# Three small edits around the first expert round: a sort product moved, slots handed on in another order, one slot more

## The chip, the core and the metric

One core of a Trainium2 chip runs the whole program. TensorE (PE) multiplies matrices and writes to PSUM banks; VectorE (DVE) and ScalarE (ACT) empty the banks; GpSimd (POOL) does some elementwise work; SyncE (SP) issues the weight transfers, and 16 DMA engines carry them. The metric is the device time of one execution in microseconds (us). The time before is the median of 3 runs.

## The reference

Two layers over 512 tokens of width 1024. Each layer mixes tokens (dilated attention, a spatial gating unit, a short convolution), then runs a mixture of 32 experts of which each token uses two of one group:

```python
def hierarchical_moe(x, wg, bg, we, be, w_gate, w_up, w_down):
    ...
    _, g_idx = lax.top_k(g_logit, 1)
    ...
    top_logit, top_local = lax.top_k(e_logit, TOP_K_INNER)
    gate = g_p * jax.nn.softmax(top_logit, -1)
    expert = g_idx * EXPERTS_PER_GROUP + top_local
    ...
    def run_block(args):
        rows, e = args
        xb = x_pad[rows]
        hdn = jax.nn.silu(xb @ w_gate[e]) * (xb @ w_up[e])
        return hdn @ w_down[e]
```

All weights are float32. An expert has three matrices of 2 MB, so the 32 experts of a layer are some 200 MB, and every one of them is read.

## The kernel before, in words

Each layer has a dense stage (`dense`, `output`) and an expert stage (`moe`). In the expert stage the experts are worked off in 13 rounds. Rounds 0 and 1 are fixed: each serves two experts that are known beforehand, 64 columns of tokens for each. Rounds 2 to 12 take the other 28 experts, in an order that the kernel finds by sorting the experts by their token counts. The sort is `keys`, `sort_a`, `sort_b`, `sort_c`: `sort_a` ranks the experts with two small products on TensorE; `sort_b` makes a table `found` on VectorE and ends with a product (L1226) that spreads it over all partitions; `sort_c` copies the result into `ids`, `base` and `cap`. `ids` tells SyncE which experts to load from round 2 on.

These steps are woven into `gather`, which collects the tokens of rounds 0 and 1 on TensorE in four quarters (L1334), each into one of two `t` banks, emptied half by ScalarE (L1345) and half by VectorE (L1343).

The weights live in slots of 1 MB. `self.free` is a list of the names of the free slots, first in, first out. `feed` takes the next entries of a fixed loading order while slots are free and issues their transfers on SyncE's queue (L362 for the experts); an issued transfer waits on the queue until the former content of its slot has been read, and all behind it wait too. `drop` and `release` give a weight's slots back to the list:

```python
    def drop(self, *keys):
        ws = [self.loaded.pop(key) for key in keys]
        for tags in zip(*(w.tags for w in ws)):
            self.give(tags)
```

Each weight has two slots, its first and its second half. The loading order of a fixed round is: first halves of gate of both experts, first halves of up, second halves of gate, second halves of up. `first(r)` is a round's product with gate and up (through `hidden`, L1374); for a fixed round `hidden` is called with `parts` ((0, 4), (4, 8)), so it reads in that same order. `second(r)` is the product with down (L1405). The program order is: gathers and sort, `first(0)`, `first(1)`, `second(0)`, the gathers of round 2 and 3, `second(1)`, and then round by round. Two further slots, named Y and Z, hold dense tiles and serve once per layer for a weight.

In the expert stage the order of all engines is as the code is written (`self.manual`); in most of the dense stage a planner of the framework orders the instructions. At the end of the dense stage `output` gives back the last dense slots and feeds.

Of the kernel before, what the change touches and what calls it, by code (L numbers as in the profile page):

```python
# [28 lines left out]
NE = 32  # L29
# [46 lines left out]
def columns(members):  # L76

    w = 64 if all((b - a) % 64 == 0 for _, a, b in members) else 32
    return [(e, c, c + w) for e, (_, a, b) in enumerate(members) for c in range(a, b, w)]
# [86 lines left out]
class Trunk:  # L166
# [4 lines left out]
    def setup(self, ctx):  # L171
        tc, nc = self.tc, self.nc
        con = ctx.enter_context(tc.tile_pool(name="con", bufs=1))
        self.slots = ctx.enter_context(tc.tile_pool(name="slots", bufs=1))
        self.ps = ctx.enter_context(tc.tile_pool(name="ps", bufs=1, space=PSUM))
        self.sm = ctx.enter_context(tc.tile_pool(name="sm", bufs=2))

        self.X = con.tile([128, NT, D], F32, name="X")
        self.fa = con.tile([128, 4, 512], FR, name="fa")
        self.f = con.tile([128, 8, 512], F32, name="f")  # L180
        self.tab = con.tile([128, NTAB - 512], F32, name="tab")
        self.ident = con.tile([128, 128], F32, name="ident")
        self.tri = con.tile([128, 128], BF, name="tri")
        self.onesb = con.tile([128, 128], BF, name="onesb")
        self.ones = con.tile([128, 128], F32, name="ones")
        self.eps = con.tile([128, 1], F32, name="eps")
        self.pp = con.tile([128, NPP], F32, name="pp")
        self.wr = con.tile([128, KT + 1, 64], F32, name="wr")
        self.rk = con.tile([128, NT, NE], F32, name="rk")
        self.G = con.tile([128, NT, NE], F32, name="G")  # L190


        self.u = con.tile([128, R0, NT], F32, name="u")
        self.Gp = con.tile([128, R0, NT], F32, name="Gp")
        self.ur = con.tile([128, 2, NT, NS], F32, name="ur")
        self.base = con.tile([128, NE], F32, name="base")
        self.ids = con.tile([128, NE], I32, name="ids")
        self.gt = con.tile([128, 2, 512], F32, name="gt")
        self.cap = con.tile([128, NE], F32, name="cap")
        self.cnt = con.tile([128, 96], I32, name="cnt")  # L200
        self.gv1 = con.tile([128, 1], F32, name="gv1")


        self.fb = self.half("fb", FR, "Y")[0]
        self.f2 = self.half("f2", F32, "Z")[0]
        m = 0
        self.iota = self.tab[:, m : m + 128]
        self.perm = self.tab[:, m + 164 : m + 196]
        self.w4 = self.tab[:, m + 128 : m + 132]
        self.w32 = self.tab[:, m + 132 : m + 164]  # L210
        col = lambda c: self.tab[0:NE, m + c : m + c + 1]
        self.t_at, self.t_base, self.t_cap, self.t_id, self.t_tie = (col(c) for c in range(196, 201))
        self.t_ties = self.tab[:, m + 201 : m + 233]
        self.t_rounds = self.tab[:, m + 233 : m + 233 + NS]

        for t in range(2):
            self.load_x(t)
        make_identity(nc, self.ident)
        nc.gpsimd.memset(self.onesb, 1.0)
        nc.gpsimd.memset(self.ones, 1.0)  # L220
        nc.gpsimd.memset(self.eps, EPS)
        nc.gpsimd.affine_select(
            out=self.tri, in_=self.onesb, pattern=[[1, 128]], compare_op=OP.is_gt,
            fill=0.0, base=0, channel_multiplier=-1,
        )
        self.free = [f"R{k}" for k in range(18)]

    def load_x(self, t):
        self.nc.sync.dma_start(self.X[:, t, :], self.i["x"][t * 128 : (t + 1) * 128, :])
# [986 lines left out]
    def sort_b(self):  # L1216

        v, rt, rp = self.nc.vector, self.rt, self.rp
        self.found = rt[0:NE, 472:568]
        at = rt[0:NE, 470:471]  # L1220
        v.tensor_copy(at, rp[0:NE, 240:241])
        row = rp[0:NE, 200:232]
        v.tensor_scalar(self.found[:, 64:96], self.iota[0:NE, 0:32], at, self.t_id, OP.is_equal, OP.mult)
        v.tensor_scalar(self.found[:, 0:32], row, self.t_at, self.t_base, OP.is_equal, OP.mult)
        v.tensor_scalar(self.found[:, 32:64], row, self.t_at, self.t_cap, OP.is_equal, OP.mult)
        self.nc.tensor.matmul(self.rp[:, 256:352], self.ones[0:NE, :], self.found, start=True, stop=True)  # L1226

    def sort_c(self):

        v, ps = self.nc.vector, self.rp[:, 256:352]  # L1230
        v.tensor_copy(self.ids, ps[:, 64:96])
        v.tensor_copy(self.base, ps[:, 0:32])
        v.tensor_copy(self.cap, ps[:, 32:64])
# [81 lines left out]
    def moe(self, l):  # L1315
        nc, f, fa = self.nc, self.f, self.fa
# [7 lines left out]
        def gather(quarters=range(4), n=2):  # L1324

            w = 128 * n
            for kk in quarters:
                ps = self.t()
                for j in range(2):
                    k = 2 * kk + j  # L1330
                    i = 0
                    for src, one in ((x1h, oh), (x1l, self.oh16)):
                        for t in range(NT):
                            nc.tensor.matmul(  # L1334
                                ps[:, w * j : w * j + w], src[:, k, 128 * t : 128 * t + 128],
                                one[:, 0:n, t, :], start=(i == 0), stop=(i == 2 * NT - 1),
                            )
                            i += 1
                for j in range(2):
                    k = 2 * kk + j  # L1340
                    src = ps[:, w * j : w * j + w]
                    if j:
                        nc.vector.tensor_scalar(xg[:, k, 0:w], src, gain(k), bias(k), OP.mult, OP.add)  # L1343
                    else:
                        nc.scalar.activation(xg[:, k, 0:w], src, AF.Identity, bias=bias(k), scale=gain(k))  # L1345
# [16 lines left out]
        def members(r):  # L1362
            return len(ROUNDS[r - R0] if r >= R0 else FIXED[r])

        def weights(r, *names):
            return [self.loaded[(l, n, r, e)] for n in names for e in range(members(r))]

        def hidden(pss, w, xs, blocks, fill=(), parts=((0, 8),)):

            fill = list(fill)  # L1370
            for m, part in [(m, part) for part in parts for m in range(len(w))]:
                for k in range(*part):
                    for e, a, b in blocks:
                        nc.tensor.matmul(  # L1374
                            pss[m][a:b, :], xs[:, k, a:b], w[m][e][:, k, :],
                            start=(k == 0), stop=(k == 7),
                        )
                    if k % 2 == 1 and fill:
                        fill.pop(0)()
# [166 lines left out]
        def release(r, *names):  # L1546
            for n in names:
                self.drop(*((l, n, r, e) for e in range(members(r))))

        def first(r, fill=(), keep=0):  # L1550

            pss = [self.g(), self.g()]
            xs = xg[:, :, 128 * (r % 2) : 128 * (r % 2) + 128]
            if r >= R0:
                for m, n in enumerate(("gate", "up")):
                    if m:
                        self.feed()
                    hidden(pss[m:], [weights(r, n)], xs, columns(ROUNDS[r - R0]), fill[4 * m : 4 * m + 4])
                    release(r, n)
            else:  # L1560
                w = [weights(r, n) for n in ("gate", "up")]
                hidden(pss, w, xs, halves, fill, ((0, 4), (4, 8)))
                release(r, "gate", "up")
            if keep == 1:
                spare.append(self.free.pop())
            held = [self.free.pop() for _ in range(4 if keep == 4 else 0)]
            self.feed()
            self.free.extend(held)
            return pss
# [23 lines left out]
        with self.manual(ET.PE, ET.SP):  # L1593

            gather((0,))
            self.sort_a()
            gather((1,))
            self.sort_b()
            gather((2,))
            self.sort_c()  # L1600
            self.known = l
            self.feed()
# [9 lines left out]
            slots = []  # L1612
            none = lambda: None
            pss = first(0, [none] * 5 + [lambda: slots.append(by_slot(0)), none, lambda: slots.append(by_slot(1))])
            h = act(pss)
            self.gates(2)
# [16 lines left out]
            for r in range(R0, NR):  # L1633
# [3 lines left out]
                n = min(2, NR - 1 - r)  # L1637
# [48 lines left out]
        n = 4 // members(NR - 1)  # L1686
# [165 lines left out]
```

## Time and profile before

| | |
|---|---|
| time before, median of 3 runs | 1522.19 us (1519.39 to 1522.41) |
| time of the profiled execution | 1520.52 us |
| its span, first to last instruction | 1518.8 us |
| TensorE busy | 1368.6 us (90%) |
| VectorE busy | 683.3 us (45%) |
| DMA, mean over the span | 293 GB/s |

The profile is of one execution. A busy time is the time in which an engine worked on any instruction. SyncE's queue (SPq) isn't counted as busy; its waits are listed apart, counted from the end of its last instruction. A wait names what ended it. PEclk is the granted TensorE clock: 1.00 is 2.4 GHz, 0.50 is 1.2 GHz.

### The profile page before, as it was taken

The numbers are of one execution on the slowest core, as the hardware profiler recorded it, in microseconds if no ns is written. First come the engines' busy times: TensorE is split into PE (matmuls) and PEld (weight loads), VectorE is DVE, ScalarE is ACT, GpSimd is POOL, SyncE is SP. The second block draws the span as 40 slices with busy tenths as digits, with TensorE's granted clock in tenths as the row PEclk, the third lists the DMA queues.
The fourth block names the chain that finished last, engine by engine and source line by source line (L and its number), as shares of the span: only waits on it lengthen the run. The fifth ranks groups of instructions, "written<-read, shape, count | busy, mean of one in ns | idle before, by whom it ended". The sixth has DMA issues, their size and how long they took to land. (4 is left out here: it accounts for less than half of the span.)

```text
span 1518.8 us, 22582 instructions
## 1 busy us (share of the span) xinstructions
PE 1368.6 (90%) x8828; PEld 750.3 (49%) x8829; DVE 683.3 (45%) x1528; ACT 397.2 (26%) x720; POOL 156.0 (10%) x190
## 2 busy tenths in 40 slices
PE   8999997999989898989699998979999898989894
PEld 7776576443434342434377665864434343433341
DVE  4347758534242424232553676585352424241325
ACT  5446544110101010101463555341101010101013
POOL 2112206000000000000141221060000000000001
PEclk9999999899999998999799998999999999999997
DMA  9410354499999999999911025444999999999994
GB/s 346 141 56 1 113 193 166 164 411 408 419 419 419 418 419 410 419 418 410 382 45 59 1 84 192 141 167 184 410 410 419 419 418 419 419 410 419 419 404 151
DMA packets 84551, 445.16 MB, mean 293 GB/s; under 512 B 8080, under 2 KB 14352, under 8 KB 36816
## 3 DMA queue, kind: packets, MB, share of 16 engines
q1 hardware_dynamic: 83184, 440.15, 72.2%
q0 software_dynamic: 960, 2.90, 0.6%
q8 instruction: 74, 1.21, 0.3%
q10 hardware_dynamic: 288, 0.52, 0.1%
q14 instruction: 45, 0.37, 0.1%
HBM read 441.45 MB, written 2.10 MB: 292 GB/s over the span
## 5 line engine op out<-in xcount | busy, mean ns | idle before, releaser
L1374 PE MATMUL g<-w,f 128*32 128x512 f32 (+1 forms) x3072 | 411.8, 602 | 36.3 <-DMA w<-expert_w_up 26.9
L1374 PEld LDWEIGHTS g<-w,f 128*32 128x32 f32 (+1 forms) x3072 | 113.6, 113 | 303.5 <-issue 220.6
L1405 PE MATMUL g<-w,f 128*32 128x512 f32 (+1 forms) x1536 | 215.4, 642 | 31.3 <-DMA w<-expert_w_down 15.6
L1405 PEld LDWEIGHTS g<-w,f 128*32 128x32 f32 (+1 forms) x1536 | 58.8, 118 | 165.0 <-issue 125.3
L1416 DVE SCALAR_TENSOR_TENSOR y<-g,gv,y 128x512 fp32r<-128x512 f32 x52 | 39.1, 751 | 208.8 <-ACT y L1415 206.4
L1428 DVE TENSOR_TENSOR X<-X,s 128x512 f32<-128x512 f32 x88 | 56.4, 683 | 127.1 <-PE s L1423 127.1
L1415 ACT ACTIVATE y<-g,gv 128x512 fp32r<-128x512 f32 x52 | 35.8, 689 | 245.0 <-PE g L1405 245.0
L1334 PE MATMUL t<-fa,mh 128*128 128x256 f32 (+1 forms) x448 | 82.8, 308 | 0.6 <-DVE f L1207 0.6
L1387 DVE TENSOR_TENSOR f<-g,f 128x512 f32<-128x512 f32 x26 | 17.9, 690 | 134.3 <-PE g L1374 130.9
L1345 ACT ACTIVATE f<-t,pp 128x256 f32<-128x256 f32 (+1 forms) x56 | 30.9, 551 | 177.1 <-PE t L1334 177.1
L1343 DVE TENSOR_SCALAR f<-t,pp 128x256 f32<-128x256 f32 (+1 forms) x56 | 29.4, 525 | 90.8 <-ACT f L1345 90.8
L1334 PEld LDWEIGHTS t<-fa,mh 128*128 128x128 f32 x448 | 62.7, 197 | 12.4 <-DVE X L1428 8.4
L1334 PE MATMUL t<-f,x1l 128*128 128x256 f16 (+1 forms) x448 | 67.5, 275 | 0.0
L1428 DVE TENSOR_TENSOR X<-X,t 128x512 f32<-128x512 f32 x88 | 56.3, 682 | 19.9 <-PE t L1423 19.9
L1423 PE MATMUL s<-y,fa 128*128 128x512 f32 x208 | 62.8, 422 | 2.4 <-ACT y L1415 1.8
L1386 ACT ACTIVATE f<-g 128x512 f32<-128x512 f32 x26 | 15.6, 598 | 188.3 <-PE g L1374 188.3
L1534 POOL DMA_DIRECT2D rows<-ln_gain x2 | 1.1, 550 | 586.9 <-PEq L1450 586.9
L1423 PEld LDWEIGHTS s<-y,fa 128*128 128x128 f32 x208 | 35.0, 188 | 51.2 <-issue 40.1
L1423 PE MATMUL t<-y,fa 128*128 128x512 f32 x208 | 59.1, 405 | 0.5 <-DVE xl L462 0.5
L1394 ACT COPY f<-s 128x512 f32<-128x512 f32 x26 | 15.2, 587 | 162.9 <-PE s L1393 135.1
L409 POOL TENSOR_TENSOR X<-X,E 128x512 f32<-128x512 f32 x11 | 16.3, 1486 | 332.5 <-ACT X L1712 168.8
L409 POOL TENSOR_TENSOR X<-X,f 128x512 f32<-128x512 f32 x32 | 40.9, 1309 | 87.8 <-DVE x1l L953 82.3
(343 smaller groups left out, 2273.8 us busy)
## 6 DMA issues: line engine op xcount, KB each, us to landing
w<-expert_w_gate SPq DMA_DIRECT2D x128, 1024.0 KB, 19.8
w<-expert_w_up SPq DMA_DIRECT2D x128, 1024.0 KB, 19.8
w<-expert_w_down SPq DMA_DIRECT2D x116, 1024.0 KB, 19.8
w<-w_in SPq DMA_DIRECT2D x20, 1024.0 KB, 13.9
w<-expert_w_down SPq DMA_DIRECT2D x48, 256.0 KB, 5.4
w<-w_out SPq DMA_DIRECT2D x8, 1024.0 KB, 5.5
X<-x SPq DMA_DIRECT2D x4, 512.0 KB, 5.8
w<-w_in SPq DMA_DIRECT2D x4, 512.0 KB, 8.1
```

Source lines behind the costliest of these rows:

```text
L409: e.tensor_tensor(out=x, in0=x, in1=row[:, 512 * h : 512 * h + 512], op=op)
L1334: nc.tensor.matmul(ps[:, w * j : w * j + w], src[:, k, 128 * t : 128 * t + 128], one[:, 0:n, t, :], start=(i == 0), stop=(i == 2 * NT - 1),)
L1343: nc.vector.tensor_scalar(xg[:, k, 0:w], src, gain(k), bias(k), OP.mult, OP.add)
L1345: nc.scalar.activation(xg[:, k, 0:w], src, AF.Identity, bias=bias(k), scale=gain(k))
L1374: nc.tensor.matmul(pss[m][a:b, :], xs[:, k, a:b], w[m][e][:, k, :], start=(k == 0), stop=(k == 7),)
L1386: nc.scalar.activation(hp, gate, AF.Silu)
L1387: nc.vector.tensor_mul(hp, up, hp)
L1405: nc.tensor.matmul(pss[hf][a:b, :], hT[:, 128 * j + a : 128 * j + b], part(e, hf, j), start=(j == 0), stop=(j == 3),)
L1415: nc.scalar.mul(yh, ps, gv)
L1416: nc.vector.scalar_tensor_tensor(yl, ps, gv, yh.bitcast(F32), OP.mult, OP.subtract)
L1423: nc.tensor.matmul(ps, oT[:, 128 * t : 128 * t + 128], y[q], start=(q == 0), stop=(q == 1))
L1428: nc.vector.tensor_add(x, x, ps)
```

## The change

Three edits. The list of slots has 19 names instead of 18; the 8 KB per partition for it come in part from a smaller scratch for the transfers that GpSimd issues (`dynamic_dma_scratch_size`, 8192 to 2048 bytes). The product of L1226 moves from the end of `sort_b` to the head of `sort_c`, and `sort_b` now stands ahead of the second quarter of the gather: TensorE's order goes from quarter 0, `sort_a`, quarter 1, product, quarter 2, quarter 3 to quarter 0, `sort_a`, quarters 1 and 2, product, quarter 3. And a fixed round gives its gate and up slots back in one `drop`, so that the list gets the first halves of gate and up before the second halves.

```diff
-        self.free = [f"R{k}" for k in range(18)]
+        self.free = [f"R{k}" for k in range(19)]
...
         v.tensor_scalar(self.found[:, 32:64], row, self.t_at, self.t_cap, OP.is_equal, OP.mult)
+
+    def sort_c(self):
+
         self.nc.tensor.matmul(self.rp[:, 256:352], self.ones[0:NE, :], self.found, start=True, stop=True)
-
-    def sort_c(self):
-
         v, ps = self.nc.vector, self.rp[:, 256:352]
...
                 hidden(pss, w, xs, halves, fill, ((0, 4), (4, 8)))
-                release(r, "gate", "up")
+                self.drop(*((l, n, r, e) for n in ("gate", "up") for e in range(members(r))))
...
             gather((0,))
             self.sort_a()
-            gather((1,))
             self.sort_b()
-            gather((2,))
+            gather((1, 2))
             self.sort_c()
...
-    nc = bacc.Bacc("TRN2", target_bir_lowering=False, num_devices=1, dynamic_dma_scratch_size=8192)
+    nc = bacc.Bacc("TRN2", target_bir_lowering=False, num_devices=1, dynamic_dma_scratch_size=2048)
```

## Rows read from the trace of the kernel before

**Rows 1.** The page: the span, and the DMA engines' busy tenths in 40 slices.
```profile
span 1518.8 us, 22582 instructions
...
DMA  9410354499999999999911025444999999999994
```

**Rows 2.** Windows: stretch, busy us (instructions) by engine, PEclk, DMA share, GB/s.
```profile
265.00:285.50 20.50, 17.83 (x103) 13.21 (x104) 8.30 (x39) 3.78 (x8) 1.00 (x2) 0.79 0.01 2
...
302.80:400.00 97.20, 96.97 (x706) 44.30 (x706) 41.17 (x86) 13.93 (x23) 0.00 (x0) 1.00 1.01 412
...
310.00:740.00 430.00, 392.00 (x2871) 163.01 (x2867) 146.33 (x287) 48.52 (x80) 1.06 (x2) 0.96 1.01 414
```

**Rows 3.** TensorE's waits, 400 to 735 us: total us, times, longest.
```profile
PE g L1374 <- DMA w<-expert_w_up: 12.5, 11, 1.5
PE g L1405 <- DMA w<-expert_w_down: 9.1, 6, 2.3
```

**Rows 4.** SyncE's waits: 284:286, 286:293, 320:345; last row 1040:1048, layer 1.
```profile
SPq L362 <- PE g L1374: 37.2, 1, 37.2
...
SPq L362 <- PE g L1374: 6.0, 1, 6.0
...
SPq L362 <- PE g L1405: 17.4, 2, 12.8
...
SPq L362 <- PE g L1374: 35.9, 1, 35.9
```

**Rows 5.** Timeline of SyncE's issues in layer 0: start us, us, count.
```profile
285.54 11.37 SPq L362 DMA_DIRECT2D w<-expert_w_down  x7
...
292.40 4.50 SPq L362 DMA_DIRECT2D w<-expert_w_down  x5
297.71 0.35 SPq L362 DMA_DIRECT2D w<-expert_w_gate  x1
...
338.18 0.90 SPq L362 DMA_DIRECT2D w<-expert_w_down  x2
...
338.74 0.33 SPq L362 DMA_DIRECT2D w<-expert_w_down  x1
```

**Rows 6.** Single issues at 285.54, 292.40, 297.71, 338.74: us to landing at the end.
```profile
w<-expert_w_down SPq DMA_DIRECT2D x1, 1024.0 KB, 5.0
...
w<-expert_w_down SPq DMA_DIRECT2D x1, 1024.0 KB, 4.9
...
w<-expert_w_gate SPq DMA_DIRECT2D x1, 1024.0 KB, 13.2
...
w<-expert_w_down SPq DMA_DIRECT2D x1, 1024.0 KB, 7.9
```

**Rows 7.** Timeline of the gather stage, layer 0: start us, us, idle before, releaser.
```profile
274.58 0.54 DVE L1343 TENSOR_SCALAR f<-t,pp 128x256 f32<-128x256 f32 x1 [2.01 <-ACT f L1345]
...
275.98 0.46 PE L1226 MATMUL g<-f,ones 32*128 32x96 f32 x2 [2.39 <-DVE f L1225]
...
281.86 4.51 PE L1374 MATMUL g<-w,f 128*64 128x512 f32 x20
```

**Rows 8.** Windows of the gather stage; the last is layer 1's.
```profile
273.56:276.97 3.41, 1.02 (x8) 0.85 (x8) 1.31 (x5) 0.57 (x1) 0.00 (x0) 1.00 0.01 2
276.98:280.39 3.41, 3.41 (x19) 2.85 (x17) 0.00 (x0) 0.57 (x1) 0.00 (x0) 0.50 0.00 0
...
1034.74:1038.15 3.41, 3.41 (x19) 2.85 (x17) 0.41 (x1) 0.57 (x1) 0.00 (x0) 0.50 0.00 0
```

**Rows 9.** TensorE's waits in layer 1, 1026 to 1040 us.
```profile
PE g L1226 <- DVE f L1225: 2.1, 1, 2.1
```

**Rows 10.** The view of line 444: who waited for it, and its loads' landings.
```profile
  ACT f L875: 7.4, 2
...
DMA to landing us min/median/max: 4.0/5.9/7.0
```

## The prediction

> **What bounds the kernel now.** I began with the page's row of DMA shares over the span: it is at its top in two long stretches and low between them [rows 1]. These stretches are the expert rounds of the two layers. The windows of layer 0 show the border: from 265 to 285.5 us the DMA engines move 2 GB/s while TensorE works, from 310 to 740 us they are full at 414 GB/s, and TensorE is busy for 392 of those 430 us [rows 2]. So one transfer of 1.0486 MB takes 1.0486/0.414 = 2.53 us there. The table of TensorE's waits from 400 to 735 us says what its idle time waits for: weights that land, 12.5 us for up and 9.1 us for down [rows 3]. Between 302.8 and 400 us TensorE itself never rests, 96.97 of 97.20 us [rows 2]; from 400 us on it runs behind the weights. The end of a layer's rounds is therefore the start of the weight stream, plus the number of transfers still to come times 2.53 us, plus the holes in the stream, plus a tail that the change leaves alone. The stream starts where SyncE's queue gets its first free slot: it sits 37.2 us in layer 0 and 35.9 us in layer 1 until `hidden` (L1374) has read the first quarter of fixed round 0 [rows 4]. All three edits act at this place.
>
> **The change part by part.**
>
> *The sort's last product.* In the gather stage TensorE stands 2.39 us before the product of L1226, because VectorE makes its operand only after the second quarter's evacuation at 274.58 us [rows 7]. In the new order VectorE's four small steps of `sort_b` come ahead of that evacuation; they are ready once the first quarter is evacuated, and the 2.01 us in which VectorE was idle ahead of 274.58 hold their 0.9 us (they ran between that evacuation's end at 275.1 and the product's start at 275.98 [rows 7]). TensorE goes on with the third quarter, then takes the product (0.46 us, as before), then the fourth. The two t banks do not hold it: the third quarter wants the bank of the first, the fourth that of the second, evacuated at 274.58 + 0.54 = 275.1 us [rows 7], earlier than TensorE gets there. The three copies of `sort_c` wait for the third quarter's evacuation on VectorE; behind them are the fourth quarter's evacuation and `gating`, which move up with TensorE all the same. SyncE's `feed` there issues nothing, as no slot is free, and the expert numbers are first needed for the gate load at 297.71 us [rows 5]. So the wait goes: 2.39 us in layer 0, 2.1 us in layer 1 [rows 9].
>
> The rest is the clock. In the stretch with the wait TensorE was busy for 1.02 of 3.41 us, and in the next 3.41 us the granted clock was 0.50, 1.2 instead of 2.4 GHz, although TensorE was busy throughout; layer 1 shows the same stretch at 0.50 [rows 8]. These were gather matmuls, so 3.41 us at half clock is work of 1.7 us. With no rest ahead of it I take the clock to stay up: 1.7 us more. If it falls all the same, the gain of this part is the wait alone. Part one moves the first matmul of the rounds, now at 281.86 us [rows 7], and with it the first released slot, by 2.4 + 1.7 = 4.1 us in layer 0 and 2.1 + 1.7 = 3.8 us in layer 1.
>
> *The nineteenth slot.* Counting through `feed`, `take` and `give`, 17 of a layer's 24 fixed transfers are issued before the stall with 18 slots (the two dense tiles Y and Z serve once as well), and 18 with 19. The extra transfer runs in the stretch where the DMA engines are idle [rows 2], so the stream after it is one transfer shorter: 2.5 us. That holds in both layers; in the dense stages the extra slot waits for an unlimited `feed`, and loads that come earlier there have no one waiting for them.
>
> *Reading order.* `hidden` reads the fixed rounds in quarters: first halves of gate, of up, second halves of gate, of up. Before, the slots go back as gate, gate, gate, gate, up, up, up, up, so the third transfer waits for the third quarter (SyncE stands 6.0 us [rows 4], until 292.40 [rows 5]) while the slots of the second quarter lie free. The cost is read from the landings. The first transfer is issued at 285.54 and lands 5.0 us later, at 290.5; the eighth is the gate load of 297.71, which lands 13.2 us later, at 310.9 [rows 5, 6]. Seven steps of 2.53 us would give 290.5 + 17.7 = 308.2, so the hole costs 2.7 us. With the new order a quarter takes (292.40 - 285.54)/2 = 3.4 us; the second quarter's slots are free at 289.0 and their first load could land at 289.0 + 4.9 = 293.9 [rows 6], before its turn at 295.6. The third quarter's, 292.40 + 4.9 = 297.3, are before theirs at 300.6. The hole closes.
>
> *What is given back.* Slot and order together put the stream 2.5 + 2.7 = 5.2 us ahead of TensorE's own timetable, and there is a later place where slots are released by TensorE: the down matrices of fixed round 1 (L1405), where SyncE already stands up to 12.8 us [rows 4]. As each transfer takes the slot of the one before it in the list, the load issued at 338.74 and landed 7.9 us later, at 346.6, now needs the slot released at 338.18; it cannot land before 338.18 + 4.9 = 343.1 [rows 5, 6]. So 3.5 of the 5.2 us survive. TensorE is full in this stretch [rows 2], so its releases move by part one alone. Past 400 us its 38 us of rest in 430 [rows 2] take the 3.5 us in.
>
> The Trainium skill, page "DMA: Bandwidth & Descriptors", section "Where 436 GB/s comes from", lets the HBM side bind loads at some 358 GB/s per core. The windows show 414 GB/s [rows 2], and the measurement decides. By the page one transfer would take an estimated 2.9 us and the slot would be worth 0.4 us more in each layer.
>
> *The smaller scratch* serves the loads that GpSimd issues. No row shows them at the new size. Those of L444 land 4.0 to 7.0 us after issue [rows 10], and I take no cost, which is what these rows show at the old size: the lower bound is nothing, the upper one is the last rival.
>
> *Sum.* Layer 0: 4.1 + 3.5 = 7.6. Layer 1: 3.8 + 3.5 = 7.3. Together 14.9 us. The profiled execution took 1520.52 us (span 1518.8), 1.7 below the median 1522.19 and inside the runs' 1519.39 to 1522.41. 1520.5 - 14.9 = 1505.6; against the median it would be 1507.3. I say 1505.5.
>
> **The rivals.**
>
> *The clock falls all the same.* TensorE also rests ahead of the gathers, and the wait may not be what costs the clock. Against it: the stretch at 0.50 comes right behind the one with the rest [rows 8]. Then part one is 2.4 and 2.1: 14.9 - 3.4 = 11.5, 1509.
>
> *A new wait for the one removed.* If the third quarter or the moved product waits on an evacuation, part one gives nothing; for it speaks that TensorE has only two t banks and VectorE empties half of each quarter; against it the bank times above. The rest is 2 x 3.5 = 7.0: 1513.5.
>
> *All of the 5.2 us is kept.* If the releases of round 1 come earlier than by part one, 2 x 1.7 = 3.4 more: 18.3, 1502.2. TensorE's full stretch speaks against it.
>
> *Hidden.* If TensorE and not the stream set the end of the rounds, nothing changes, 1520.5. For it: 392 of 430 us busy [rows 2]. Against it: the rest is waits for weights [rows 3].
>
> *Slower: GpSimd's loads in pieces.* ScalarE's scaling at L875 waits 7.4 us in two for the row load of L444 [rows 10], and ScalarE's evacuations for the output stage are queued behind it. If a scratch of a quarter cuts that load into four pieces, each waiting for the last to land, it lands 3 x 7.0 = 21 us later in each layer; TensorE waits for those evacuations, and the time is 1520.5 - 14.9 + 42 = 1548. It decides from 7.5 us of delay per layer on. Against it: at the old size the same loads show no sign of pieces, 4.0 to 7.0 us being about what SyncE's loads take (5.0 and 4.9 us [rows 6]).
>
> The Trainium skill, page "SBUF — State Buffer", section "SBUF size: 192, 224, or 256?", has 16 KiB per partition set aside for these descriptor rings, which speaks against 2 KiB. No run here shows that size; before ran with 8 KiB and the landings above.
>
> **How the numbers follow.** Forecast 0.60; clock falls 0.13; new wait 0.09; all kept 0.06; hidden 0.06; slower 0.06. The range takes in the forecast, the clock, the new wait and the larger gain, with a spread of 1 to 2 us between executions: 1501 to 1514. About 0.2% (3 us) is what a measurement here can tell from no change; faster holds 0.60 + 0.13 + 0.09 + 0.06 = 0.88, same 0.06, slower 0.06.
>
> **What the changed profile would show.** Part one: no wait before L1226, granted clock 1.00 through the fourth quarter, the first L1374 of the rounds 4 us earlier against the gathers' start. Slot: two down loads instead of one before the stall. Order: SyncE's 6.0 us wait after the first release shrinks to about 3, and the loads behind it land every 2.53 us. Given back: a longer wait on L1405 near the release of round 1's down slots. It would be wrong if TensorE waited less for weights past 400 us and the rounds still ended no earlier, if the dense stages, which a planner orders and in which every slot name moves by one, came out longer, or if L875 waited longer.

## The result, and the profile after

The changed kernel took 1511.18 us (median of 4 runs, 1507.70 to 1512.29), the kernel before beside it 1521.45 us (4 runs). The ratio is 0.993, 95% interval [0.991, 0.9951]: 7.5 to 13.7 us faster. The prediction said 1505.5 us in a range of 1501 to 1514. The profiled execution is that of 1512.29 us, the slowest of the four, with a span of 1510.5.

The gather stage first. Windows of layer 0 (columns as in [rows 2]), in the place of [rows 8]:

```profile
271.82:275.23 3.41, 3.41 (x31) 2.88 (x28) 1.31 (x5) 0.56 (x1) 0.00 (x0) 0.99 0.02 5
275.24:278.65 3.41, 3.41 (x29) 2.87 (x27) 1.20 (x5) 1.13 (x2) 0.00 (x0) 1.00 0.01 2
278.65:282.06 3.41, 3.41 (x22) 1.68 (x22) 1.65 (x10) 0.87 (x3) 0.00 (x0) 1.00 0.00 0
```

The timeline of the same stretch, in the place of [rows 7] (the product now stands in L1229), and TensorE's waits from 268 to 284 us, all that there are:

```profile
270.43 1.19 PE L1334 MATMUL t<-fa,mh 128*128 128x256 f32 x4 [0.27 <-DVE f L1207]
...
277.25 0.46 PE L1229 MATMUL g<-f,ones 32*128 32x96 f32 x2
...
279.69 4.51 PE L1374 MATMUL g<-w,f 128*64 128x512 f32 x20
```

```profile
PE t L1334 <- DVE f L1207: 0.3, 1, 0.3
```

From the second to the fourth quarter TensorE is busy without a gap, the product has no wait, and the granted clock stays at 2.4 GHz (the first quarter still begins at the low clock, as the 1.19 us of its first four matmuls show). From the first gather matmul to the first matmul of the rounds it takes 9.26 us where before took 13.47.

Now SyncE, in the place of [rows 4]: the waits from 282 to 284, from 284 to 291 and from 318 to 345 us. In the block below them are the landings of single issues, at 283.37 (the first into a handed-on slot), 330.35, 336.00 and 336.58 us, in the place of [rows 6].

```profile
SPq L362 <- PE g L1374: 32.2, 1, 32.2
...
SPq L362 <- PE g L1374: 4.8, 2, 2.6
...
SPq L362 <- PE g L1405: 17.4, 2, 12.8
```

```profile
w<-expert_w_down SPq DMA_DIRECT2D x1, 1024.0 KB, 5.0
...
w<-expert_w_down SPq DMA_DIRECT2D x1, 1024.0 KB, 4.9
...
w<-expert_w_down SPq DMA_DIRECT2D x1, 1024.0 KB, 5.0
...
w<-expert_w_down SPq DMA_DIRECT2D x1, 1024.0 KB, 8.1
```

The wait of 6.0 us became two of 2.6 and 2.2. The wait of 12.8 us for the down matrices of round 1 is unchanged, and now the two loads issued when it and the next one end (330.35 and 336.00) land 4.9 and 5.0 us later, about the least that an expert load of 1 MB took in any profile here (4.8). Before, the load issued at the end of the wait of 12.8 us took 5.8.

To see what the stream of weights kept of its gains, I count a layer's 210 expert loads in their order and take for each the time from the first issue into a handed-on slot to its landing. The *lead* is how much less that is than for the same load of before. Part one does not enter it; the other two edits do. (Each value is a difference of landing times of the trace; layer 0, layer 1.)

| kernel | 25th load | 36th | 39th | 41st | last |
|---|---|---|---|---|---|
| changed kernel | 4.3, 4.5 | 4.3, 4.3 | 3.4, 1.0 | 2.6, 1.2 | 2.8, 1.0 |
| changed kernel, again | 4.2, 4.3 | 4.2, 4.4 | 3.4, 3.3 | 2.4, 2.4 | 2.3, 2.7 |
| scaling moved | 4.4, 4.2 | 4.4, 4.3 | 3.5, 3.2 | 2.6, 1.9 | 2.6, 1.7 |
| move alone | -0.1, 0.0 | -0.2, -0.1 | -0.1, 0.0 | 0.2, 0.3 | 0.1, 0.4 |
| slot and scratch alone | 2.4, 2.6 | 2.4, 2.1 | 3.2, 2.3 | 2.4, 2.4 | 2.7, 2.8 |
| order alone | 1.7, 1.9 | 0.2, 1.1 | -0.2, 0.0 | -0.1, -0.4 | 0.1, 0.7 |
| late gather added | 4.3, 4.5 | 4.2, 4.4 | 5.1, 4.8 | 3.8, 3.7 | 3.7, 3.9 |
| late gather, scaling moved | 4.3, 4.4 | 4.0, 4.4 | 4.9, 4.8 | 3.9, 3.9 | 3.9, 3.7 |
| late gather, old order | 2.5, 2.6 | 2.2, 2.5 | 3.1, 2.9 | 3.5, 3.4 | 2.8, 3.4 |

In the changed kernel the lead is 4.3 us by the 25th load, falls from the 37th to the 41st, which is where the load issued at 330.35 and those behind it land, and is some 2.5 us from there to the end; in layer 1 of this profile it is only 1.0 to 1.3. (In the rows of the scaling, explained below, an instruction of the dense stage moved. "Scaling moved" has the slots, the order and the gathers of the changed kernel, so it shows the same stream a third time.)

The profiled pair can be added up. Layer 0: gather 4.2 and lead 2.8, but the gather began at 270.4 us and not at 268.4: 5.0. Layer 1: gather 3.8 and lead 1.0, but from layer 0's last landing to layer 1's first gather matmul it took 295.4 us and not 291.9: 1.4 (from the unrounded times). After the last landing it took 25.0 us and not 26.9: 1.9. Together 8.3, and so much the spans differ. So in this one execution the dense stages took back 5.5 us that the edits had given.

One place where layer 0's dense stage lost time is seen in the same window of before and of the changed kernel:

```profile
176.00:187.00 11.00, 9.98 (x47) 6.00 (x48) 8.12 (x22) 8.23 (x15) 1.23 (x4) 0.84 0.21 71
```

```profile
176.00:187.00 11.00, 10.14 (x29) 6.07 (x30) 6.86 (x19) 6.16 (x12) 0.62 (x3) 0.53 0.23 94
```

TensorE was about as busy, but at a mean granted clock of 0.53 instead of 0.84, and got through 29 matmuls instead of 47.

### The profile page after: what moved, and what is told of

The parts are those of the page before. It is cut to its first block, busy times and chain, and to the rows that moved or that the text cites. A ratio compares the mean times of both kernels' runs of the same rounds, so it can differ in the third digit from the quotient of the medians.

```text
span 1510.5 us, 22583 instructions
## 1 busy us (share of the span) xinstructions
PE 1364.1 (90%) x8828; PEld 747.9 (50%) x8829; DVE 683.5 (45%) x1528; ACT 396.2 (26%) x720; POOL 155.4 (10%) x190
## 5 line engine op out<-in xcount | busy, mean ns | idle before, releaser
L1374 PEld LDWEIGHTS g<-w,f 128*32 128x32 f32 (+1 forms) x3072 | 111.2, 113 | 304.4 <-issue 223.1
L1405 PE MATMUL g<-w,f 128*32 128x512 f32 (+1 forms) x1536 | 211.5, 631 | 31.0 <-DMA w<-expert_w_down 15.5
L1405 PEld LDWEIGHTS g<-w,f 128*32 128x32 f32 (+1 forms) x1536 | 58.0, 117 | 161.4 <-issue 122.3
L1334 PEld LDWEIGHTS t<-fa,mh 128*128 128x128 f32 x448 | 60.9, 192 | 12.1 <-DVE X L1428 8.4
```

Source lines behind the costliest of these rows:

```text
L1334: nc.tensor.matmul(ps[:, w * j : w * j + w], src[:, k, 128 * t : 128 * t + 128], one[:, 0:n, t, :], start=(i == 0), stop=(i == 2 * NT - 1),)
L1374: nc.tensor.matmul(pss[m][a:b, :], xs[:, k, a:b], w[m][e][:, k, :], start=(k == 0), stop=(k == 7),)
L1405: nc.tensor.matmul(pss[hf][a:b, :], hT[:, 128 * j + a : 128 * j + b], part(e, hf, j), start=(j == 0), stop=(j == 3),)
```

## The experiments

Batches ran at different times, each beside runs of before of its own (medians 1522.26, 1522.29 and 1522.67 us).

**Move alone** (the product moved, nothing else):

```diff
+
+    def sort_c(self):
+
         self.nc.tensor.matmul(self.rp[:, 256:352], self.ones[0:NE, :], self.found, start=True, stop=True)
-
-    def sort_c(self):
-
...
             gather((0,))
             self.sort_a()
-            gather((1,))
             self.sort_b()
-            gather((2,))
+            gather((1, 2))
             self.sort_c()
```

> The sort's product alone is moved; 18 slots, old order, old scratch. Theory A (the wait and the half clock behind it are what the move removes, and the stream's start passes it on in full): from the first gather matmul to the first L1374 of the rounds 9.3 us as in the changed kernel, against 13.5 before; every landing 4 us earlier in layer 0 and 8 us earlier in layer 1; about 1513 us, 8 us under before, if the dense stages take as long as before. Theory B (the wait's place is taken by later waits, and what the changed kernel gained came from the slot and the order): under 3 us gained. The dense stage of layer 0 should end where it does before (first gather matmul near 268.4 us) by the theory that the 19th slot lengthens it, and anywhere from 268 to 271 by the theory that the granted clock's steps do.

Measured: 1515.61 us (12 runs), ratio 0.9951 [0.9931, 0.997], 6.7 us less than before. The gather took 8.67 us in layer 0 (13.47 before) and 10.48 in layer 1 (13.08). In layer 1 the whole first quarter ran at the low clock; the timeline has its groups of four matmuls at 1.20 and 1.08 us, later ones at 0.73 and 0.61:

```profile
1027.22 1.19 PE L1334 MATMUL t<-fa,mh 128*128 128x256 f32 x4 [0.92 <-DVE fa L1294]
1028.21 1.08 PE L1334 MATMUL t<-f,x1l 128*128 128x256 f16 x4
1028.94 1.20 PE L1334 MATMUL t<-fa,mh 128*128 128x256 f32 x4
...
1035.26 0.46 PE L1229 MATMUL g<-f,ones 32*128 32x96 f32 x2
1035.64 0.73 PE L1334 MATMUL t<-fa,mh 128*128 128x256 f32 x4
1036.22 0.61 PE L1334 MATMUL t<-f,x1l 128*128 128x256 f16 x4
```

This low clock is not that of the wait. The windows of the same layer show a stretch at 0.50 that began ahead of the gather, and the full clock from there to the rounds:

```profile
1024.70:1031.50 6.80, 5.88 (x27) 4.66 (x27) 2.62 (x13) 1.57 (x3) 0.13 (x1) 0.50 0.01 2
1031.52:1037.70 6.18, 6.18 (x51) 5.20 (x50) 2.70 (x10) 1.30 (x3) 0.00 (x0) 1.00 0.00 0
```

Before has such a stretch too, from 263.3 us in layer 0 and 1021.1 in layer 1, also 6.8 us long. How much of it falls into the gather differs: 1.7 and 1.6 us in before's two layers, 0.1 and 4.3 with the move alone. That is why the two layers came out above and below the forecast of 4.1 and 3.8; the stretch behind the wait is gone in both.

The lead stays near nothing, so the edit moves the start of the rounds and does not touch the stream behind it. Its 4.8 + 2.6 = 7.4 us of gather agree with the runs.

**Slot and scratch alone:**

```diff
-        self.free = [f"R{k}" for k in range(18)]
+        self.free = [f"R{k}" for k in range(19)]
...
-    nc = bacc.Bacc("TRN2", target_bir_lowering=False, num_devices=1, dynamic_dma_scratch_size=8192)
+    nc = bacc.Bacc("TRN2", target_bir_lowering=False, num_devices=1, dynamic_dma_scratch_size=2048)
```

> The 19th slot and the small scratch alone; the product where it was, old order. Theory A: the stream is one transfer shorter in each layer and keeps its hole of the third transfer: first release at the same distance from the gathers as before (17.2 us from the first gather matmul), landings 2.5 us earlier from then on in each layer; about 1516 us, 5 under before, if the dense stages are equal. Theory B: the 19th slot moves the dense stage's transfers and names and makes the dense stages longer by 2 us in layer 0 and 3 in layer 1, as seen in the changed kernel's profile; then the first gather matmul starts near 270.4 us and the time is 1520 to 1522, no gain.

Measured: 1520.28 us, ratio 0.9978 [0.996, 0.9996]. The lead is 2.4 and 2.6 us at the 25th load and 2.7 and 2.8 at the end. TensorE's wait ahead of the product stood as in [rows 7]:

```profile
PE g L1226 <- DVE f L1225: 2.4, 1, 2.4
```

Two leads of 2.75 would be 5.5 us; the runs show 0.6 to 6.1, and the medians differ by 2.0. So the size of this part rests on the lead; the times only do not contradict it.

**Order alone:**

```diff
-                release(r, "gate", "up")
+                self.drop(*((l, n, r, e) for n in ("gate", "up") for e in range(members(r))))
```

> The slots of fixed rounds in reading order alone; 18 slots. Theory A (what closes the hole is given back at the down slots of round 1): SyncE's wait of 6.0 us behind the first release shrinks to about 3, the load that landed at 310.9 lands 2.7 us earlier, but behind the release of round 1's down slots at most 0.9 us of it is left: 1519 to 1521 us, 0 to 2 under before. Theory B (nothing is given back, the hole is worth its full size): 2.7 us in each layer, 5.4 us under before, 1516.

Measured: 1522.51 us, ratio 0.9997 [0.9979, 1.0015]: nothing. SyncE's waits from 287.5 to 296 us, the first line below, show that the edit does its work, for the 6.0 us became two waits, the longer of 2.6, and the lead is 1.7 and 1.9 us at the 25th load. It is gone at the 39th. SyncE's waits from 330 to 346 us, the second line, show the two places at L1405 where it waits as before:

```profile
SPq L362 <- PE g L1374: 5.2, 2, 2.6
```

```profile
SPq L362 <- PE g L1405: 17.4, 2, 12.8
```

With 18 slots the load that leaves when the wait of 12.8 us ends is the 36th. Before, it landed 5.8 us after its issue, so it could come no more than about 0.9 us sooner (a load that finds the queues empty took 4.9), and the lead at that load is 0.2 and 1.1.

**Scratch alone:**

```diff
-    nc = bacc.Bacc("TRN2", target_bir_lowering=False, num_devices=1, dynamic_dma_scratch_size=8192)
+    nc = bacc.Bacc("TRN2", target_bir_lowering=False, num_devices=1, dynamic_dma_scratch_size=2048)
```

> The scratch alone, 2048 for 8192 bytes, 18 slots. Theory A: no cost, 1520 to 1522 us, the row loads of L444 land 4 to 7 us after issue, and L875 waits 7 to 8 us in two. Theory B (GpSimd's loads wait for room in the smaller ring): landings over 8 us, L875 waits over 12 us in two, and the time is 4 us or more above before, which would be part of the gap between the forecast and the changed kernel.

Measured: 1522.30 us, ratio 0.999 [0.9973, 1.0007]: the scratch costs nothing that can be measured. The row loads of L444 landed after

```profile
DMA to landing us min/median/max: 3.8/6.8/8.0
```

up to 1.0 us later than before [rows 10], and the scaling at L875 waited 9.1 us in two for them where before waited 7.4. The scratch need not be the cause: with the move alone, at the old size, they took up to 9.6 us and the wait was 10.6. The Trainium skill, page "SBUF — State Buffer", section "SBUF size: 192, 224, or 256?", sets 16 KiB aside for these descriptors; here 2 KiB was enough.

**The changed kernel again**, to see how far one profile can be trusted:

> The changed kernel itself once more, beside the kernel before. The parts measured one by one gave about 7 us for the move, 2 to 3 for the slot and nothing for the order. Theory A (the parts add up, and the order's gain is given back): 9 to 11 us under before; the stream from the first released slot to its last landing 446 us, as with the slot alone, in both layers. Theory C (the order is worth something beside the slot that it is not worth alone, since the slot moves the later releases): 12 to 14 us under before, and the stream 444 us. In either theory the stretch from layer 0's last landing to layer 1's first gather matmul tells whether the 19th slot lengthens layer 1's dense stage (295 us again, as in two profiles with 19 slots) or chance does (anything from 291 to 296).

Measured: 1510.02 us (6 runs), ratio 0.9919 [0.9897, 0.9942]. The gather took 9.49 and 9.20 us, layer 0's gather began at 269.5, and from layer 0's last landing to layer 1's gather it was 291.8 us, as before. So the 3.5 us lost there in the first profile are not lost each time. That the change makes a long stretch likelier is not ruled out: over all profiles it was 291.7 to 292.5 us in the four with 18 slots and 291.7 to 295.7 in the nine with 19. The same sum as above gives 4.0 + 3.9 + 2.3 + 2.7 less 1.1, plus 0.3 for the rest: 12.1, which is the difference of the spans (1518.8 and 1506.7). The time lies where Theory C put it, the streams (446.5 and 446.1 us) where Theory A did; the interval of the time, 8.8 to 15.7 us, holds both, so the streams decide.

**Late gather.** If the lead is lost because round 1's down slots come free no earlier, an earlier release of them must keep it. The changed kernel with the last two quarters of the gather of rounds 2 and 3 behind `second(1)` instead of ahead of it:

```diff
-            gather((2, 3))
             oT, gv = slots[1]
             some, _ = several(steps, (0, 0, 4, 0, 0, 4))
             steps = spreads(1, oT, second(1, gv, some))
+            gather((2, 3))
```

> The changed kernel with the last two gather quarters of rounds 2 and 3 put behind the product of round 1 with down, so that round 1's down slots come free some 3.7 us earlier; the same work otherwise. Theory A (the order's gain is given back at these slots): SyncE's wait of 12.8 us on L1405 falls to about 9, the holes at the two releases close, and the stream from the first release to the last landing takes 444 to 445 us instead of 446 in each layer: 2 to 4 us under the changed kernel. Rival (the hole comes back at the next release, or the lost time is transfers of instructions that share the engines): the stream stays at 446, and the time within 1 us of the changed kernel, or above it by TensorE's new pause before the product.

Measured: 1509.84 us, ratio 0.9908 [0.9889, 0.9927]. In the stream it did what the theory says. SyncE's waits from 325 to 349 us:

```profile
SPq L362 <- PE g L1405: 14.4, 2, 9.9
SPq L362 <- PE g L1374: 6.9, 1, 6.9
```

The wait of 12.8 us is 9.9, and the load issued at its end landed 7.0 us later instead of 4.9: its slot no longer limits it. The lead is 5.1 and 4.8 us at the 39th load. At the 41st, issued at the end of the 6.9 us and landing 5.0 us later, it falls to 3.8, because the moved gather delays the next releases. It ends 1.2 to 1.3 us a layer above that of the changed kernel's repeat. The 2.5 us that this makes in two layers lie inside the intervals: by their times (1509.84 and 1510.02 us) the two kernels cannot be told apart.

**Late gather with the old order:**

```diff
-                self.drop(*((l, n, r, e) for n in ("gate", "up") for e in range(members(r))))
+                release(r, "gate", "up")
```

> The product moved, 19 slots, the late gather of the rounds, but slots handed on in the order of before. Theory (reading order closes a hole early in the stream, and the gain survives only with the late gather): the stream stays near 446.2 us a layer, so order with late gather is worth about 1.2 us a layer. Rival (the late gather itself gives the 1.2 us): 445 us without the reading order.

Measured: 1507.98 us (4 runs), ratio 0.9904 [0.988, 0.9928]. The lead ends at 2.8 and 3.4 us, the streams are 446.1 and 445.4 us. Neither theory has the whole: against the slot alone (2.7, 2.8) the late gather by itself brings 0.1 and 0.6 us, and the order adds 0.9 and 0.5 to it. In time the order is worth nothing that can be measured, with the late gather and 19 slots or alone with 18. The changed kernel without the order was not run.

**The dense stage.** The gather of layer 0 began anywhere from 268.2 to 278.0 us in the 13 profiles, more than the edits are worth there. I suspected the row load of L444: ScalarE waits for it at L875 [rows 10], and TensorE's waits for ScalarE lie behind that. First the scaling of L875 on GpSimd instead of ScalarE, without and with the late gather:

```diff
-        nc.scalar.mul(tabs[0], tabs[0], 1.0 / UP)
+        nc.gpsimd.tensor_scalar(tabs[0], tabs[0], 1.0 / UP, None, OP.mult)
```

> The changed kernel with the scaling of the row load (L875) on GpSimd instead of ScalarE, so that ScalarE's copies for the attention do not stand behind the landing of that load. Theory D (the dense stages of the 19-slot kernels are longer because this load lands behind one more weight transfer, ScalarE stands 5 us in layer 1, TensorE 3.7 us behind it at L735, and the clock falls longer): the wait of TensorE on L722 goes below 2 us, the stretch from layer 0's last landing to layer 1's first gather matmul falls from 295 to 291 us or less, the first gather matmul of layer 0 comes 1 to 3 us earlier, and the time is 4 to 7 us under the changed kernel. Theory E (the stretches differ by the phase of the clock's steps alone): the dense stages vary as before and the time is within 2 us of the changed kernel.

> Both edits of the two runs above on the changed kernel. If both theories hold, their gains add up: 6 to 11 us under the changed kernel, near 1502 us; if only the row load's place counts, 4 to 7 under; if neither, within 2 us of it.

Measured: 1516.81 us, ratio 0.9959 [0.9941, 0.9977], and with the late gather 1515.95 us, 0.995 [0.993, 0.997]: some 6 us above the same kernels without it. No theory had them slower. The line's view, without the late gather, shows what GpSimd did (columns: shortest, median and longest in ns, then first and last start):

```profile
L875 POOL TENSOR_SCALAR f<-f x2: 2776/2786/2795, 196.1 to 944.9; 128x1024 f32<-128x1024 f32 x2
its engine sat idle before it (us, times) until:
  DMA f<-ln_gain: 12.0, 2
```

GpSimd takes 2.79 us where ScalarE took 1.06, and it stands still for 12.0 us in two. TensorE's waits (160 to 270 us) show a new one, behind VectorE:

```profile
PE t L796 <- DVE E L746: 4.1, 1, 4.1
```

Second, the scaling on ScalarE as before, but written further down, behind the output stage's first pass:

```diff
-        nc.scalar.mul(tabs[0], tabs[0], 1.0 / UP)
...
         A = nc.scalar
+        A.mul(tabs[0], tabs[0], 1.0 / UP)
```

> The changed kernel with one instruction moved: the scaling of the input by ln_gain stays on ScalarE but stands behind the first of the dense stage's other ScalarE work instead of ahead of it. Theory (the row load's landing, 6.1 to 9.95 us after its issue, blocks ScalarE, and everything queued behind it there is late): ScalarE no longer stands at the scaling, TensorE's waits for ScalarE in that stage (up to 3.7 us in layer 0, 2.5 to 3.8 us in layer 1) shrink below 1 us, the first gather matmul of layer 0 begins by 269 us, and the time is 2 to 6 us below the changed kernel's. Rival (another wait or the clock takes the place, as with the scaling on GpSimd): within 2 us of the changed kernel, or above it.

> The scaling moved back on ScalarE, and also the gather of the second and third quarter's rounds behind the second product of the round before. If both theories hold: as the run with the scaling alone in the dense stage, and the stream of weights 445 us a layer from the first handed-on slot to the last landing instead of 446.3, so about 2 us less than that run. Rival: the streams are 445 us, but the time is that of the other run within 1 us, because what the stream gains lies below what the dense stages vary by.

Measured: 1510.17 us, ratio 0.9929 [0.9906, 0.9952], and with the late gather 1508.82 us, 0.9903 [0.9883, 0.9922]. The first is the changed kernel's time within 0.2 us of its repeat: the rival holds. In the line's view (scaling now L914) the scaling still starts at 195.3 us (195.5 in before) and ScalarE still stands there, for the planner left it in its old place, between the copies of L722 and L742:

```profile
L914 ACT ACTIVATE f<-f x2: 1056/1058/1061, 195.3 to 940.2; 128x1024 f32<-128x1024 f32 x2
...
  DMA f<-ln_gain: 7.6, 2
```

So this run did not take the suspected wait away, and it neither proves nor clears the row load. The profiles themselves speak for it. In layer 0 ScalarE stood 2.9 to 4.1 us ahead of the scaling in six of the eleven profiles with the scaling on ScalarE, and the gather began at 268.2 to 270.4 us; in the other five it stood 4.4 to 6.4 us, and the gather began at 273.2 to 276.9. The copy of L743 stands behind the scaling on ScalarE, and TensorE's wait for it (190 to 212 us) is 0.2 to 1.4 us in the six and 1.7 to 3.7 in the five, which alone then have a stretch of 3.4 to 6.8 us at 0.50 that begins between 199.6 and 203.7 us. Below are this wait in the changed kernel's repeat and in the late gather, and the window of that stretch in the late gather:

```profile
PE g L889 <- ACT E L743: 0.9, 1, 0.9
...
PE g L889 <- ACT E L743: 3.7, 1, 3.7
...
203.80:210.50 6.70, 6.70 (x19) 5.44 (x19) 2.10 (x3) 3.64 (x6) 0.00 (x0) 0.50 0.45 157
```

Layer 1 sorts the same way: 3.9 to 4.6 us ahead of the scaling go with 291.7 to 293.0 us from layer 0's last landing to the gather, 5.1 and 5.2 us (the first profile of the changed kernel, the slot alone) with 295.4 and 295.7. Of layer 0's five, two have 18 slots. This is a pattern over single profiles and not a test. It was not tried to bring that load in earlier or to leave the scaling out. With the late gather added, the stream ends 445.0 and 445.1 us after its first handed-on slot, as expected, and the time is 1.35 us lower, inside the intervals.

No version beat the changed kernel by more than can be measured; the three with the late gather and the scaling on ScalarE have the lowest medians, 1507.98 to 1509.84.

## Why the prediction was right, and which term was off

**The move** was sized right: forecast 4.1 and 3.8 us, measured 4.2 and 3.8 (4.0 and 3.9 in the repeat). Both halves of it held, the wait and the clock: without the wait no stretch at 0.50 follows. That the clock falls all the same is refuted by the windows above, and a new wait in its place by the list of waits. One thing was missing: the gather's length also depends on how much of the earlier stretch at 0.50 falls into it. By an estimate from these rows (counted at half, because the clock is half there) the 1.6 us less and 2.7 us more of it that the move alone has against before turn 4.1 and 3.8 into 4.9 and 2.5; measured were 4.8 and 2.6.

**The slot** was sized right: forecast 2.5 us a layer, lead of 2.4 to 2.8 from the 41st load on with the slot alone.

**Order and what is given back** is the step that was off. I took 2.7 us for the hole that the order closes, 5.2 with the slot, and let 3.5 survive. The lead with both edits was 4.3, so the order closed 1.8. The rest of the 2.7 is no hole of the slots. The fourth load into a handed-on slot was issued at 287.24 and landed only at 296.96, 9.7 us later, a step of 3.58 us behind the third, in which the DMA engines were full. The windows from the third landing on, in the changed kernel:

```profile
293.38:296.96 3.58, 3.58 (x20) 1.31 (x18) 1.95 (x4) 0.00 (x0) 0.00 (x0) 1.00 1.02 419
296.96:299.45 2.49, 2.49 (x14) 0.90 (x12) 2.46 (x9) 0.00 (x0) 0.00 (x0) 1.00 1.01 421
```

Before has such a step there too, from 297.27 to 300.88, and I had counted it as hole: seven steps of the 2.49 us that the second line shows leave 2.9 us of before's 20.4 from the first landing to the eighth, and 2.9 less the 1.1 by which that one step is too long is 1.8.

The amount given back, forecast 1.7 us, was 1.7 to 1.9 in four of the six layers of the three profiles of this stream (3.3 in layer 1 of the first, where the 39th load came 4.95 us behind the 38th although it was issued 7.5 us ahead of its landing; 2.4 in layer 1 of "scaling moved"), and at the place named, but only for half of it is the reason named shown. The sign that I gave did not come: the wait on L1405 is no longer than before, 12.8 us. What grew is the step to the landing of the load that it holds, 2.50 us before and 3.38 in the changed kernel. The lead fell to 3.4 at the 39th load, as the bound of 3.5 said, and the late gather, which moves the releases of round 1's down slots, shows that these set it. The other 0.8 to 1.0, up to the 41st, do not come from a slot that came free late: the 40th load was issued at 336.58, 8.1 us ahead of its landing, and still came 3.63 us behind the 39th. Whether the release has a part in that is not shown: with the late gather, where no load was held up at this place, the 40th came 2.47 us behind the 39th. The bound could also have been read with 18 slots, where it leaves the order 0.9 us: the order by itself was never worth its hole.

So some 2.5 us a layer survive instead of 3.5 (1.0 and 1.7 in the two layers named). That is no more than the slot alone keeps: in the changed kernel the order is worth nothing at the end of the stream. The sum is 4.1 + 2.5 + 3.8 + 2.5 = 12.9 us instead of 14.9. In the repeat the medians differ by 12.3 us, in the first measurement by 10.3 (7.5 to 13.7, so that 14.9 lies outside). What remains of the difference, as far as the profiled pair shows it, is in the dense stages, whose length the prediction took as fixed and which vary by several us between executions. Two of its signs of being wrong did come in the first profile: the dense stages were 5.5 us longer, and L875 waited 8.0 us instead of 7.4.

That the time lies inside the range is in part luck. The range reached up to 1514 for the sake of two rivals, the clock and the new wait, and neither came; the loss in the dense stages had no term.

**The other rivals.** "All kept" and "hidden" are out. Past 400 us TensorE rests for weights almost as long as before in the changed kernel (11.9 us for up and 9.0 for down, against 12.5 and 9.1 [rows 3]), so the stream and not TensorE still sets the end. GpSimd's loads in pieces did not come: the scratch alone cost nothing.

The Trainium skill's 358 GB/s (page "DMA: Bandwidth & Descriptors", section "Where 436 GB/s comes from") is again not what bounds this stream; the window from 310 to 740 us shows 412 GB/s:

```profile
310.00:740.00 430.00, 388.66 (x2864) 162.21 (x2858) 149.76 (x297) 51.17 (x86) 1.06 (x2) 0.97 1.01 412
```

## What to carry to other kernels

A short rest of one engine can cost more than its length, because the granted clock may fall behind it; removing it by letting independent work go first was the largest part here (6.7 us of some 12). When a stream of loads is put ahead of its consumer, look for the next place where buffers come free by the consumer's own timetable, in each version by itself: the gain is cut there to the slack that the load behind that release has over its shortest landing. Judge edits of 1 or 2 us by the distance between two events on both sides of the edit, as long as other stages vary by more than that.

## What the runs showed that was not expected

Lone steps of 3.0 to 4.2 us instead of 2.5 between landings, of loads issued well before, stand at like places in layer 0 of all 13 profiles: one ends at the 46th to 48th load, one at the 101st or 102nd, one at the 147th to 149th. Those of layer 1 stand elsewhere. In the changed kernel, layer 0, such steps, of about 3.6 us, end at the 22nd, 40th, 47th, 101st and 148th load. In each of them, or in the step before, the DMA view has one packet on an instruction queue. From 293.38 to 296.96 and from 338.00 to 341.02 us it shows

```profile
q8 instruction: 1, 0.02, 1.8%
```

```profile
q8 instruction: 1, 0.02, 2.0%
```

which is 1.8% of 16 engines over 3.58 us, 1.0 us of one engine, and 1.0 us again: about the 1.1 us by which the steps are too long. If a load is spread over all engines, it would land only when the late one is done. This is argued from coincidence and not shown, for 26 such packets fall into that stream and only five go with a long step.

The dense stage's granted clock differs between executions with the same work: it sat at 0.50 for 3.4 us from 178.0 us on before, for 10.2 us from 176.3 on in the first profile of the changed kernel and for 6.8 us from 175.8 on in its repeat. What starts the longer stretches at this place stayed open.
